# Hybrid SSD/gMLP step on one core: splits of v spread over more turns, x·dt·decay made on VectorE, weight sums begun later, product evictions at a higher priority, and four smaller moves

## The chip, the core and the metric

The kernel runs on one NeuronCore of a Trainium2 chip. The metric is the device time of one execution in microseconds (us). A core has five engines with a queue of instructions each: TensorE (PE in the rows, its weight loads PEld), VectorE (DVE), ScalarE (ACT), GpSimd (POOL) and SyncE (SP), which here only issues DMAs. Each works its own list of instructions in order and waits on semaphores for the others.

## The reference, cut to what matters

One layer, `DEPTH = 1`, over a prompt of 4096 rows and a sample of 32 rows, width 1024, all in f32:

```python
h = rms_norm(x, g_pre) * (1 + scale[:, None]) + shift[:, None]
z, xbc, dt_raw, u, v, gt = jnp.split(h @ w_in, [i1, i2, i3, i4, i5], axis=-1)
xbc, conv_new = causal_conv(xbc, conv_prev, conv_w, conv_b)      # width 4, then silu
dt = jax.nn.softplus(dt_raw + dt_bias)
y, ssm_new = ssd_scan(xs, dt, a, bm, cm, ssm_prev)               # 16 heads of 64, state 128
ssd_out = (y + d_skip[:, None] * xs).reshape(bsz, L, SSD_WIDTH) * jax.nn.silu(z)
v_n = layer_norm(v, g_v, beta_v)
gmlp_out = jax.nn.silu(gt) * u * gmlp_spatial(v_n, w_s, b_s)     # 8 groups of 128 channels
mix = jnp.concatenate([ssd_out, gmlp_out], axis=-1) @ w_out
out = x + gate[:, None] * rms_norm(mix, g_post)
```

Inside the scan a chunk's contribution to the state is `einsum(B, decay_end * dt, x)`, and the part within the chunk is `einsum((C·B) * decay, dt * x)`.

## The kernel before, in words

**Blocks and steps.** The prompt is worked in 8 blocks of 512 rows (`NB`, block index b). A block has a first step (k = 0, which makes B and C), then the output products of the block before (`out_proj`), then the products that make v (`v_stage`), then eight more steps (k = 1 to 8), each of which makes two column tiles from `w_in`: pairs of heads ("p", x and z) and groups of the gMLP branch ("g", gate and u). The sample's 32 rows ride along in block 3, and with block 4's output products. Blocks 0 and 1 use plain products (`plain_step`, `v_plain`); from block 2 on (`FROM`) the steps are done with seven products on sums of parts of the matrices instead of eight (`super_step`, `STEPS`, `LEAVES`). Every f32 operand is held as two f16 parts, and a product is three f16 products; `split` makes the two parts (ACT copies the high part, POOL or DVE subtracts for the low one).

**Weights.** In block 0 the weights are loaded in f32, scaled, split and written back to DRAM as f16 tiles. The sums of parts that the later blocks need are made in block 1 by 22 jobs (`sums_load`, `sums_scale`, `sums_first`, `sums_second`, `sums_third`, `sums_split`): DMA in, some sums on DVE, splits on ACT and POOL or DVE, DMA out from POOL's queue.

**Turns and priorities.** The order of the work is written out by hand: `later(n, fn)` puts a function n turns ahead, and `tick()`, called some 14 to 16 times in a step, starts whatever is due. What a function emits then has its place in the program; a list scheduler orders each engine's instructions by that place (the priority) among those that it holds to be ready by its own estimates. `shifted(n, fn)` emits at a priority moved by n places (negative is earlier), `behind` is `shifted(200)`, used for the sums. What the scheduler writes is then fixed: on the chip each engine keeps that order.

**A pair of heads.** When its product leaves PSUM, `conv` makes xsT on DVE (L815, L818) and `silu` follows on ACT (L805). `pair_xt` turns it on PE into rows (ps_xt, L1152). `pair_xdt` multiplies by dt on DVE (xdt<-ps_xt), one turn later `pair_xde` multiplies xdt by the decay on POOL (xde<-xdt, both L1167). `pair_state` (ps_s, L1175) needs xde; `pair_y` (ps_y, L1208) needs xdt and the masked decay L, which comes from a DMA'd row (L1124), Relu and Exp on ACT (L1134, L1139) and the mask on POOL (L1145).

**v.** `v_norm` finds mean and scale of the rows, then for chunk c of four `later(3 * c, v_split)` and per half of 512 columns `v_split_half`: vt on DVE (L1078), one turn later `split` (ACT L274, POOL L275). Half 0 is first needed by group 0 in step 2, half 1 by group 4 in step 6.

**Products leaving PSUM.** In `super_step` `leave` copies a finished product with its scale on ACT (L731), or adds it on DVE (L729); the next product but one into the same PSUM bank has to wait for it. In `plain_step` ACT does so (L757).

**Others that the change touches.** The start's bound `a_sc`, from the largest |gcol| and |scol| (L644 to L663: six DVE steps, a transpose and a product on PE, four more on DVE). `out_proj`'s end of a half: the sample's product is turned back to rows (`by_token`) right behind it, L967 to L970, and then all streams leave PSUM (L1414, L1416). `finish` for the prompt (conv and SSM states, L1435 to L1454), emitted ahead of the last `finalize_mix`. The start turns of the 22 sums jobs, `places` (L1634, L1635).

Of the kernel before, what the change touches and what calls it, by code (L numbers as in the profile page):

```python
# [18 lines left out]
P = 128  # L19
# [57 lines left out]
def hybrid_step_kernel(ctx: ExitStack, tc: tile.TileContext, io: dict, out: list):  # L77
# [566 lines left out]
    bnd = const.tile([P, 2, KT], F32, name="bnd")  # L644
    bnd2 = const.tile([P, 2, KT], F32, name="bnd2")
    nc.vector.tensor_scalar(bnd, gcol, math.sqrt(DM), None, op0=ALU.mult)
    nc.vector.tensor_single_scalar(bnd.bitcast(I32), bnd.bitcast(I32), 0x7FFFFFFF, op=ALU.bitwise_and)
    nc.vector.tensor_single_scalar(bnd2.bitcast(I32), scol.bitcast(I32), 0x7FFFFFFF, op=ALU.bitwise_and)
    nc.vector.tensor_tensor(bnd, bnd, bnd2, op=ALU.add)
    bmx = const.tile([P, 1], F32, name="bmx")  # L650
    nc.vector.tensor_reduce(bmx, bnd, axis=AX.XY, op=ALU.max)
    ps = psum("ps_bmx")
    nc.tensor.transpose(ps[0:1, 0:P], bmx, ident)
    bm1 = const.tile([1, 1], F32, name="bm1")
    nc.vector.tensor_reduce(bm1, ps[0:1, 0:P], axis=AX.X, op=ALU.max)
    nc.vector.tensor_scalar_max(bm1, bm1, 2.0 ** -40)
    ps = psum("ps_bm1")
    nc.tensor.matmul(ps[:, 0:1], ones[0:1, :], bm1, start=True, stop=True)
    e_i = const.tile([P, 1], I32, name="e_i")
    nc.vector.tensor_copy(e_i.bitcast(F32), ps[:, 0:1])  # L660
    nc.vector.tensor_single_scalar(e_i, e_i, 23, op=ALU.logical_shift_right)
    nc.vector.tensor_scalar(a_sc.bitcast(I32), e_i, -B23, (127.0 + 12 + 127) * B23, op0=ALU.mult, op1=ALU.add)
    nc.vector.tensor_scalar(a_inv.bitcast(I32), e_i, B23, -12.0 * B23, op0=ALU.mult, op1=ALU.add)  # L663
# [60 lines left out]
    def leave(s, ps, dst, scale):  # L724

        j, t, adds = LEAVES[s]
        d, sc = dst(j, t), scale(j)
        if adds:
            nc.vector.scalar_tensor_tensor(d, ps, sc, d, op0=ALU.mult, op1=ALU.add)  # L729
        else:  # L730
            nc.scalar.activation(d, ps, AF.Identity, scale=sc)  # L731
# [4 lines left out]
    def plain_step(k):  # L736

        ws = None
        for j in (1, 0):
            ps = [psum("ps_proj") for _ in range(2)]  # L740
            for kh in range(2):
# [3 lines left out]
                for pi in range(2):  # L745
# [9 lines left out]
                    if kh:  # L755
                        c = 4 * k + 2 * pi + j
                        nc.scalar.activation(ws[pi].d[j], ps[pi], AF.Identity, scale=scw[:, c:c + 1])  # L757
                        done(prompt, ws[pi], j)
# [114 lines left out]
    def dt_cumsum(st, e):  # L873
# [17 lines left out]
        nc.scalar.activation(st.de, st.de, AF.Exp)  # L891
        later(9, dt_rows, st)
# [152 lines left out]
    def v_norm(st, mv):  # L1045
# [15 lines left out]
        for c in range(n):  # L1061
            later(3 * c, v_split, st, c, mv, r)
# [4 lines left out]

    def v_split(st, c, mv, r):
        Q = st.Q
        sp = st.v[c].bitcast(F16).rearrange("p (h a d) -> p h a d", h=2, a=2)  # L1070
        for half in range(2):
            later(half, v_split_half, st, c, half, sp, mv, r)
        st.vsplit.append(sp)

    def v_split_half(st, c, half, sp, mv, r):
        Q = st.Q
        t = tmp2(prompt, "vt")[0:Q]
        nc.vector.tensor_scalar(t, st.v[c][0:Q, half * 512:half * 512 + 512], mv[0:Q, c, 0:1],  # L1078
                                r[:, c:c + 1], op0=ALU.subtract, op1=ALU.mult)
        later(1, split, sp[0:Q, half, 0], sp[0:Q, half, 1], t, nc.gpsimd)  # L1080
# [75 lines left out]
    def pair_xdt(st, j, w, ps):  # L1156
        Q, n, nm = st.Q, st.nch, st.name
        w.xdt = wk.tile([P, n, P], F32, tag="xdt" + nm, name="xdt", bufs=1)[0:Q]
        pair_times(st, j, nc.vector, w.xdt, ps[0:Q, 0:n * P].rearrange("q (c m) -> q c m", c=n), st.dt)
        later(1, shifted, -150, pair_xde, st, j, w)  # L1160

    def pair_xde(st, j, w):
        w.xde = wk.tile([P, st.nch, P], F32, tag="xde" + st.name, name="xde", bufs=1)[0:st.Q]
        pair_times(st, j, nc.gpsimd, w.xde, w.xdt, st.de)
# [215 lines left out]

    def out_proj(active, first, final=False):
# [7 lines left out]
        for half in range(1 if final else 2):  # L1389
# [4 lines left out]
            for st in active:  # L1394
                ps[st] = [psum("ps_out") for _ in range(st.nch)]
            if sample in active:
                ps_t = psum("ps_outT")
            for k2 in range(8):
# [6 lines left out]
                if k2 < 7:  # L1405
                    yield
            if sample in active:
                by_token(ps[sample][0], ps_t[:, 0:4 * TS], ps_t[:, 4 * TS:8 * TS])
            for st in active:
                if half == 0:  # L1410
                    st.o = [big("o") for _ in range(st.nch)]
                for c in range(st.nch):
                    osl = st.o[c][0:st.Q, half * 512:half * 512 + 512]
                    nc.scalar.activation(osl, ps[st][c][0:st.Q], AF.Square,  # L1414
                                         accum_out=st.os[0:st.Q, c, half:half + 1])
                    nc.scalar.activation(osl, ps[st][c][0:st.Q], AF.Copy)  # L1416
# [183 lines left out]
    for b in range(NB):  # L1600
# [30 lines left out]
        if b == 1:  # L1631

            f = region(0, "sums").rearrange("p i a k t -> p (i a k t)").bitcast(F32)
            places = [(18 + 18 * n, f[:, 0:3072]) for n in range(10)]  # L1634
            places += [(27 + 18 * n, f[:, 3072:6144]) for n in range(9)]  # L1635
# [39 lines left out]
    finish(prompt, conv_p[0, 0])  # L1675
    for st in prev:
        finalize_mix(st)
    tick()
# [33 lines left out]
```

## Time and profile before

| | |
|---|---|
| median of 3 runs | 3073.78 us (3070.44 to 3076.58) |
| the profiled execution: its own time | 3074.91 us |
| its span in the trace | 3073.2 us |
| mean granted TensorE clock | 0.972 |
| busy: PE / DVE / ACT / POOL | 92% / 57% / 50% / 42% |

The span runs from the first to the last instruction; 1.7 us lie around it. A granted clock of 1 is 2.4 GHz, one of 0.5 is 1.2 GHz. Idle time of an engine that is not the bottleneck costs nothing by itself. In the rows "L778" is line 778 of the kernel, "ps_s<-xde,bt" is what an instruction writes and reads by the program's names.

### The profile page before, as it was taken

What the parts mean: (1) busy time and instruction counts of PE and PEld (TensorE: products, weight loads), DVE (VectorE), ACT (ScalarE), POOL (GpSimd) and SP (SyncE); (2) the same over time, 40 slices, a digit from 0 to 9 for tenths busy, and PEclk for the clock granted to TensorE, in tenths of its full rate; (3) what the DMA queues carried; (4) which work ended last, traced back from release to release, by engine and by line L of the source; (5) the groups of instructions that cost most, each with busy time, mean ns of one, the idle gap of its engine ahead of it and who ended that gap; (6) DMA issues with size and microseconds to landing.
All of it is one profiled execution on the core that took longest, in us unless ns stands there. A gap on an engine that the chain in (4) does not pass through costs nothing.

```text
span 3073.2 us, 54218 instructions
## 1 busy us (share of the span) xinstructions
PE 2830.3 (92%) x20754; PEld 1881.3 (61%) x20754; DVE 1746.7 (57%) x3808; ACT 1529.6 (50%) x3234; POOL 1281.7 (42%) x1193
## 2 busy tenths in 40 slices
PE   7989898688999999989998999999999999999987
PEld 2434443344655887458874588747885588648863
DVE  4768686775664556355564554735455544526452
ACT  4577654567653554436544355444544354415531
POOL 2456654576632443224542245323543254204540
PEclk8999999899999999999999999999999999999999
DMA  9766468876435665265562666546663666556652
GB/s 316 237 211 199 146 203 297 267 240 212 151 104 201 200 195 177 90 205 178 179 201 75 215 201 195 176 155 211 192 214 102 222 195 188 182 173 198 197 159 57
DMA packets 269053, 577.36 MB, mean 188 GB/s; under 512 B 27898, under 2 KB 115170, under 8 KB 268792
## 3 DMA queue, kind: packets, MB, share of 16 engines
q1 hardware_dynamic: 246840, 500.86, 51.5%
q0 software_dynamic: 21952, 73.04, 6.4%
q8 instruction: 162, 2.65, 0.4%
q14 instruction: 99, 0.81, 0.1%
HBM read 499.82 MB, written 73.97 MB: 187 GB/s over the span
## 4 chain that ended last, share of the span: by engine, by line
PE 42%; DVE 12%; ACT 8%; DMA 5%; POOL 5%; issue 2%; SPq 0%; POOLq 0%; ACTq 0%; DVEq 0%
PE ps_proj L778 18%; PE ps_out L951 11%; PE ps_v L1016 5%; DMA wm<-vd 2%; DVE ms L1289 2%; DMA L<-acdp 2%; PE ps_y L1208 2%; PE ps_s L1175 1%; DVE vt L1078 1%; PE ps_out L1375 1%; POOL acc L1102 1%; POOL mix L1242 1%; PE ps_o L1212 1%; ACT L805 1%; DMA E<-acdp 1%
## 5 line engine op out<-in xcount | busy, mean ns | idle before, releaser
L778 PE MATMUL ps_proj<-hTp,wt 128*128 128x256 f16 x9072 | 1047.4, 274 | 44.6 <-ACT zs L731 26.5
L778 PEld LDWEIGHTS <-wt 128*128 128x128 f16 x9072 | 887.6, 98 | 157.2 <-issue 41.2
L951 PE MATMUL ps_out<-wm,mix 128*128 128x512 f16 x2880 | 646.2, 382 | 29.3 <-DVE dep L889 15.3
L951 PEld LDWEIGHTS <-mix 128*128 128x128 f16 x2880 | 280.9, 98 | 356.7 <-issue 28.1
L749 PE MATMUL ps_proj<-hTp,wt 128*128 128x512 f16 x1728 | 401.8, 389 | 2.5 <-DMA wt<-wd 2.5
L749 PEld LDWEIGHTS <-wt 128*128 128x128 f16 x1728 | 171.3, 100 | 203.0 <-issue 20.1
L1134 ACT ACTIVATE L<-L,acp 128x128 f32<-128x128 f32 x512 | 166.8, 391 | 165.6 <-DMA L<-acdp 150.5
L1016 PE MATMUL ps_v<-wm,hTp 128*128 128x512 f16 x1008 | 222.6, 381 | 17.8 <-DMA wm<-vd 17.8
L1224 POOL TENSOR_TENSOR mix<-mix,E 128x512 f32<-128x512 f32 x64 | 95.5, 1492 | 308.4 <-DVE E L1220 308.4
L1145 POOL TENSOR_TENSOR L<-L,cb 128x512 f32<-128x512 f32 (+1 forms) x144 | 168.1, 1180 | 104.7 <-ACT L L1139 103.0
L729 DVE SCALAR_TENSOR_TENSOR xp<-ps_proj,scw,xp 128x256 f32<-128x256 f32 x132 | 62.4, 480 | 233.5 <-PE ps_proj L778 221.5
L1016 PEld LDWEIGHTS <-hTp 128*128 128x128 f16 x1008 | 98.7, 98 | 139.2 <-issue 22.1
L818 DVE SCALAR_TENSOR_TENSOR xsT<-xp,cols,xsT 128x512 f32<-128x512 f32 (+1 forms) x216 | 182.8, 849 | 1.7
L275 POOL TENSOR_TENSOR mix<-ms,mix 128x512 f16<-128x512 f32 x64 | 90.8, 1421 | 220.6 <-ACT mix L274 220.6
L1102 POOL TENSOR_TENSOR acc<-acc,sq 128x512 f32<-128x512 f32 (+1 forms) x126 | 148.3, 1178 | 43.9 <-ACT sq L1098 42.4
L275 POOL TENSOR_TENSOR v<-vt,v 128x512 f16<-128x512 f32 (+1 forms) x66 | 83.7, 1297 | 174.9 <-ACT v L274 174.8
L275 POOL TENSOR_TENSOR hTp<-ta,hTp 128x512 f16<-128x512 f32 x60 | 71.3, 1189 | 202.7 <-ACT hTp L274 202.6
L810 ACT ACTIVATE halo_p<-xp 128x3 f32<-128x3 f32 x96 | 19.5, 203 | 220.5 <-DVE xp L729 219.9
L1167 POOL TENSOR_TENSOR xde<-xdt,dep 128x512 f32<-128x512 f32 x64 | 70.8, 1107 | 138.1 <-DVE xdt L1167 129.2
L274 ACT ACTIVATE mix<-ms 128x512 f16<-128x512 f32 x128 | 79.5, 627 | 83.4 <-DVE ms L1289 82.7
L1175 PE MATMUL ps_s<-xde,bt 128*128 128x128 f32 (+1 forms) x528 | 79.5, 296 | 41.2 <-POOL xde L1167 41.2
L1098 ACT ACTIVATE sq<-mix 128x512 f32<-128x512 f32 x120 | 74.8, 626 | 78.4 <-POOL mix L1242 59.0
(428 smaller groups left out, 4703.9 us busy)
## 6 DMA issues: line engine op xcount, KB each, us to landing
wt<-wd SPq DMA_DIRECT2D x414, 512.0 KB, 4.1
wm<-od SPq DMA_DIRECT2D x104, 512.0 KB, 3.5
wm<-vd SPq DMA_DIRECT2D x92, 512.0 KB, 4.9
L<-acdp SPq DMA_DIRECT2D x128, 256.0 KB, 4.1
sums<-in_w_in_dram SPq DMA_DIRECT2D x38, 512.0 KB, 6.5
wd<-wt POOLq DMA_DIRECT2D x36, 512.0 KB, 4.8
stg<-in_w_in_dram SPq DMA_DIRECT2D x64, 256.0 KB, 5.2
E<-acdp SPq DMA_DIRECT2D x128, 128.0 KB, 4.4
```

Of the source, the lines that this page charges most:

```text
L274: nc.scalar.activation(hi, src, AF.Copy)
L275: eng.tensor_tensor(lo, src, hi, op=ALU.subtract)
L749: nc.tensor.matmul(ps[pi].rearrange("p (h t) -> p h t", h=2), wt[:, pi, a, q * P:(q + 1) * P], prompt.h[:, 2 * kh:2 * kh + 2, b, q, :], st ...
L778: nc.tensor.matmul(ps, wt[:, pi, a, q * P:(q + 1) * P], prompt.h[:, slot, b, q, :], start=(starts and h == 0 and n == 0), stop=(n == 11), ...
L818: nc.vector.scalar_tensor_tensor(dst, xp[:, k:k + Ts], w(k), dst, op0=ALU.mult, op1=ALU.add)
L951: nc.tensor.matmul(ps[c], x(kk, a, c), w[:, kk, b, :], start=(first and n == 0), stop=(last and n == 5))
L1016: nc.tensor.matmul(ps, prompt.h[:, slot, a, q, i * P:(i + 1) * P], wt[q // 2][:, q % 2, b, :], start=(starts and n == 0), stop=(n == 11), ...
L1102: eng.tensor_tensor(st.accb if last else st.acc, st.acc, sq, op=ALU.add)
L1134: nc.scalar.activation(L[:, c, :], L[:, c, :], AF.Relu, scale=-1.0, bias=st.ac[:, c, 2 * j + hh:2 * j + hh + 1])
L1145: nc.gpsimd.tensor_tensor(w.L[hh], w.L[hh], st.cb[j // 4][0:st.Q], op=ALU.mult)
L1175: nc.tensor.matmul(ps_s[:, c * P:(c + 1) * P], st.bt[j // 4][0:st.Q, c, :], w.xde[:, c, :], start=True, stop=True)
L1224: nc.gpsimd.tensor_tensor(w.m, w.m, w.E, op=ALU.add)
```

## The change

It has eight parts. (1) `pair_xdt` makes both products on DVE straight from PSUM: xde first, with dd = decay times dt, which `dt_cumsum` makes with one multiply in place in `st.de`, then xdt; `pair_xde` on POOL goes. (2) The splits of v are put at turns 4(c + 4·half) for the prompt (0 to 28; 0 and 4 for the sample), halves 0 of all chunks first, and the split two turns behind vt instead of one. (3) `leave` and `plain_step`'s ACT copies are emitted with `shifted(-200)`. (4) The 19 sums jobs of region 0 start at turns 40 to 184 and 48 to 176, each 16 apart, instead of 18 to 180 and 27 to 171, each 18 apart. (5) `out_proj` emits the sample's turning back three turns later at the first half (at once at the second), and the prompt leaves PSUM without it. (6) The prompt's `finish` comes 8 turns later, behind `finalize_mix`. (7) The bound at the start is the root of a sum of squares: two ACT squares with accumulation, one add, one cast, one product on PE, four DVE steps. (8) The sample's ps_out tile is taken from PSUM only when it is turned back.

```diff
-    bnd = const.tile([P, 2, KT], F32, name="bnd")
...
-    nc.vector.tensor_scalar(a_sc.bitcast(I32), e_i, -B23, (127.0 + 12 + 127) * B23, op0=ALU.mult, op1=ALU.add)
-    nc.vector.tensor_scalar(a_inv.bitcast(I32), e_i, B23, -12.0 * B23, op0=ALU.mult, op1=ALU.add)
+    sq2 = const.tile([P, 2], F32, name="sq2")
+    sqj = const.tile([P, 2, 2 * KT], F32, name="sqj")
+    for i, (t, f) in enumerate(((gcol, math.sqrt(2 * DM)), (scol, math.sqrt(2.0)))):
+        nc.scalar.activation(sqj[:, i], t.rearrange("p s k -> p (s k)"), AF.Square, scale=f, accum_out=sq2[:, i:i + 1])
+    nc.vector.tensor_tensor(sq2[:, 0:1], sq2[:, 0:1], sq2[:, 1:2], op=ALU.add)
+    pow2_of_ssq(ssq_total(sq2[:, 0:1]), [P, 1], "wp", a_sc, a_inv)
@@ leave
-            nc.vector.scalar_tensor_tensor(d, ps, sc, d, op0=ALU.mult, op1=ALU.add)
+            shifted(-200, nc.vector.scalar_tensor_tensor, d, ps, sc, d, ALU.mult, ALU.add)
-            nc.scalar.activation(d, ps, AF.Identity, scale=sc)
+            shifted(-200, nc.scalar.activation, d, ps, AF.Identity, 0.0, sc)
@@ plain_step
-                        nc.scalar.activation(ws[pi].d[j], ps[pi], AF.Identity, scale=scw[:, c:c + 1])
+                        shifted(-200, nc.scalar.activation, ws[pi].d[j], ps[pi], AF.Identity, 0.0, scw[:, c:c + 1])
@@ dt_cumsum
+        nc.vector.tensor_tensor(st.de, st.de, st.dt, op=ALU.mult)
+        st.dd = st.de
@@ v_norm, v_split_half
-            later(3 * c, v_split, st, c, mv, r)
+            for half in range(2):
+                later((4 if st is prompt else 1) * (c + 4 * half), v_split_half, st, c, half, sp, mv, r)
-            later(half, v_split_half, st, c, half, sp, mv, r)
-        later(1, split, sp[0:Q, half, 0], sp[0:Q, half, 1], t, nc.gpsimd)
+        later(2, split, sp[0:Q, half, 0], sp[0:Q, half, 1], t, nc.gpsimd)
@@ pair_xdt
-        pair_times(st, j, nc.vector, w.xdt, ps[0:Q, 0:n * P].rearrange("q (c m) -> q c m", c=n), st.dt)
-        later(1, shifted, -150, pair_xde, st, j, w)
-        pair_times(st, j, nc.gpsimd, w.xde, w.xdt, st.de)
+        src = ps[0:Q, 0:n * P].rearrange("q (c m) -> q c m", c=n)
+        pair_times(st, j, nc.vector, w.xde, src, st.dd)
+        pair_times(st, j, nc.vector, w.xdt, src, st.dt)
@@ out_proj
+    def sample_out(half, ps_t):
+        ps = psum("ps_out")
+        by_token(ps, ps_t[:, 0:4 * TS], ps_t[:, 4 * TS:8 * TS])
+        out_leave(sample, half, [ps])
...
-                by_token(ps[sample][0], ps_t[:, 0:4 * TS], ps_t[:, 4 * TS:8 * TS])
+                later(3 if half == 0 else 0, sample_out, half, ps_t)
+            out_leave(prompt, half, ps[prompt])
@@ sums, end
-            places = [(18 + 18 * n, f[:, 0:3072]) for n in range(10)]
-            places += [(27 + 18 * n, f[:, 3072:6144]) for n in range(9)]
+            places = [(40 + 16 * n, f[:, 0:3072]) for n in range(10)]
+            places += [(48 + 16 * n, f[:, 3072:6144]) for n in range(9)]
-    finish(prompt, conv_p[0, 0])
     for st in prev:
         finalize_mix(st)
+    later(8, finish, prompt, conv_p[0, 0])
```

`out_leave` holds the two ACT instructions per chunk that `out_proj` had inline (a square with accumulation and a copy).

## Rows read from the trace of the kernel before

**Rows 1.** The page: busy us, share of the span and instructions by engine.
```profile
PE 2830.3 (92%) x20754; PEld 1881.3 (61%) x20754; DVE 1746.7 (57%) x3808; ACT 1529.6 (50%) x3234; POOL 1281.7 (42%) x1193
```
**Rows 2.** Waits of PE, whole span: who, whom; us in total, times, longest.
```profile
PE ps_s L1175 <- POOL xde L1167: 41.2, 11, 6.6
PE ps_xt L1152 <- ACT xsT L805: 38.1, 7, 22.6
PE ps_proj L778 <- ACT zs L731: 26.5, 21, 1.7
...
PE ps_out L951 <- DVE dep L889: 15.3, 4, 12.7
PE ps_out L970 <- DVE byt L968: 8.9, 2, 8.1
...
PE ps_proj L778 <- DVE xp L729: 7.1, 5, 1.4
...
PE ps_f L1440 <- DVE hk L1438: 5.7, 1, 5.7
```
**Rows 3.** Windows of blocks 0 and 1: busy us by engine, granted clock, DMA share, GB/s.
```profile
0.00:395.00 395.00, 350.55 (x1785) 168.11 (x1786) 271.50 (x565) 255.39 (x524) 206.83 (x204) 0.94 0.68 220
395.00:830.00 435.00, 364.81 (x1933) 185.28 (x1932) 312.86 (x514) 258.12 (x443) 249.29 (x253) 0.93 0.70 229
```
**Rows 4.** Waits of PE in block 1 (395 to 830 us).
```profile
PE ps_s L1175 <- POOL xde L1167: 27.1, 5, 6.6
```
**Rows 5.** Timeline, a pair of block 0: start, us, instruction, [idle before <-releaser].
```profile
221.88 0.68 DVE L1167 TENSOR_TENSOR xdt<-ps_xt,dtp 128x512 f32<-128x512 f32 x1
...
228.45 0.80 PE L1175 MATMUL ps_s<-xde,bt 128*128 128x128 f32 x2 [5.38 <-POOL xde L1167]
```
**Rows 6.** Timeline, a pair of block 1.
```profile
661.52 0.68 DVE L1167 TENSOR_TENSOR xdt<-ps_xt,dtp 128x512 f32<-128x512 f32 x1
...
663.39 0.97 PE L1175 MATMUL ps_s<-xde,bt 128*128 128x128 f32 x5 [4.58 <-POOL xde L1167]
```
**Rows 7.** Instructions of line 1167: count, duration ns min/median/max, first and last start.
```profile
L1167 DVE TENSOR_TENSOR xdt<-ps_xt,dtp x64: 678/692/693, 181.0 to 2940.2; 128x512 f32<-128x512 f32 x64
L1167 POOL TENSOR_TENSOR xde<-xdt,dep x64: 1037/1049/1492, 183.2 to 2943.2; 128x512 f32<-128x512 f32 x64
```
**Rows 8.** Timeline of block 1 behind the products of v.
```profile
604.95 0.67 ACT L757 ACTIVATE xp<-ps_proj,scw 128x512 f32<-128x512 f32 x1
...
612.68 1.11 PE L1152 MATMUL ps_xt<-ident,xsT 128*128 128x128 f32 x4 [22.63 <-ACT xsT L805]
```
**Rows 9.** Instructions of line 1078, as in rows 7.
```profile
L1078 DVE TENSOR_SCALAR vt<-v,mvp,nrp x64: 529/1366/5212, 153.0 to 2781.6; 128x512 f32<-128x512 f32 x64
```
**Rows 10.** Timeline of block 1's output products.
```profile
471.70 2.72 PE L951 MATMUL ps_out<-wm,mix 128*128 128x512 f16 x6 [12.66 <-DVE dep L889]
```
**Rows 11.** Window of block 1, sums tiles alone: busy DVE, ACT, POOL, then as rows 3.
```profile
395.00:830.00 435.00, 112.05 (x133) 67.53 (x95) 91.29 (x114) 0.93 0.70 229
```
**Rows 12.** Timeline of a step of block 5.
```profile
2188.65 5.40 PE L778 MATMUL ps_proj<-hTp,wt 128*128 128x256 f16 x48
...
2195.28 0.46 ACT L731 ACTIVATE zs<-ps_proj,scw 128x256 f32<-128x256 f32 x1
...
2195.78 1.47 PE L778 MATMUL ps_proj<-hTp,wt 128*128 128x256 f16 x12 [1.73 <-ACT zs L731]
```
**Rows 13.** Timeline of block 5 behind the products of v.
```profile
2095.30 7.95 DVE L1078 TENSOR_SCALAR vt<-v,mvp,nrp 128x512 f32<-128x512 f32 x8
...
2114.11 0.70 PE L1152 MATMUL ps_xt<-ident,xsT 128*128 128x128 f32 x4 [2.10 <-ACT xsT L805]
```
**Rows 14.** Timeline of the start.
```profile
47.10 0.17 DVE L640 SCALAR_TENSOR_TENSOR gcol<-gcol,cols 128x16 f32<-128x16 f32 x1
...
55.41 0.14 DVE L662 TENSOR_SCALAR a_sc<-e_i 128x1 int32<-128x1 int32 x1
```
**Rows 15.** Timeline of the end, ahead of the last output products.
```profile
2966.04 1.91 PE L1451 MATMUL ps_f<-ident,Hp 128*128 128x128 f32 x8
```

More of the change, by code (lines that the diff above doesn't have):

```diff
@@ L642, in hybrid_step_kernel @@
                                    op0=ALU.add, op1=ALU.mult)
-    bnd = const.tile([P, 2, KT], F32, name="bnd")
[L645 to L661, printed above, removed]
-    nc.vector.tensor_scalar(a_sc.bitcast(I32), e_i, -B23, (127.0 + 12 + 127) * B23, op0=ALU.mult, op1=ALU.add)
-    nc.vector.tensor_scalar(a_inv.bitcast(I32), e_i, B23, -12.0 * B23, op0=ALU.mult, op1=ALU.add)
+    sq2 = const.tile([P, 2], F32, name="sq2")
[4 more added lines that the diff above has]
+    pow2_of_ssq(ssq_total(sq2[:, 0:1]), [P, 1], "wp", a_sc, a_inv)
     nc.vector.tensor_scalar(gcol, gcol, a_sc, None, op0=ALU.mult)
@@ L1061, in v_norm @@
         for c in range(n):
-            later(3 * c, v_split, st, c, mv, r)
+            sp = st.v[c].bitcast(F16).rearrange("p (h a d) -> p h a d", h=2, a=2)
+            st.vsplit.append(sp)
+            for half in range(2):
+                later((4 if st is prompt else 1) * (c + 4 * half), v_split_half, st, c, half, sp, mv, r)
         if st is sample:
@@ L1066, in v_norm @@
                 later(4 + 2 * g, sample_spatial, g)
[L1068 to L1071, printed above, removed]
-            later(half, v_split_half, st, c, half, sp, mv, r)
-        st.vsplit.append(sp)
     def v_split_half(st, c, half, sp, mv, r):
@@ L1157, in pair_xdt @@
         Q, n, nm = st.Q, st.nch, st.name
-        w.xdt = wk.tile([P, n, P], F32, tag="xdt" + nm, name="xdt", bufs=1)[0:Q]
-        pair_times(st, j, nc.vector, w.xdt, ps[0:Q, 0:n * P].rearrange("q (c m) -> q c m", c=n), st.dt)
-        later(1, shifted, -150, pair_xde, st, j, w)
-    def pair_xde(st, j, w):
-        w.xde = wk.tile([P, st.nch, P], F32, tag="xde" + st.name, name="xde", bufs=1)[0:st.Q]
-        pair_times(st, j, nc.gpsimd, w.xde, w.xdt, st.de)
+        w.xdt, w.xde = [wk.tile([P, n, P], F32, tag=t + nm, name=t, bufs=1)[0:Q] for t in ("xdt", "xde")]
+        src = ps[0:Q, 0:n * P].rearrange("q (c m) -> q c m", c=n)
+        pair_times(st, j, nc.vector, w.xde, src, st.dd)
+        pair_times(st, j, nc.vector, w.xdt, src, st.dt)
     def pair_times(st, j, eng, dst, src, f):
@@ L1379, in out_last_half, with out_leave @@
             yield
+    def out_leave(st, half, ps):
+        for c in range(st.nch):
+            osl = st.o[c][0:st.Q, half * 512:half * 512 + 512]
+            nc.scalar.activation(osl, ps[c][0:st.Q], AF.Square, accum_out=st.os[0:st.Q, c, half:half + 1])
+            nc.scalar.activation(osl, ps[c][0:st.Q], AF.Copy)
+    def sample_out(half, ps_t):
+        ps = psum("ps_out")
+        by_token(ps, ps_t[:, 0:4 * TS], ps_t[:, 4 * TS:8 * TS])
+        out_leave(sample, half, [ps])
     def out_proj(active, first, final=False):
@@ L1393, in out_proj @@
                     st.gp = gate_row(st)
-            for st in active:
-                ps[st] = [psum("ps_out") for _ in range(st.nch)]
+            ps[prompt] = [psum("ps_out") for _ in range(prompt.nch)]
             if sample in active:
@@ L1406, in out_proj @@
                     yield
+            if half == 0:
+                for st in active:
+                    st.o = [big("o") for _ in range(st.nch)]
             if sample in active:
-                by_token(ps[sample][0], ps_t[:, 0:4 * TS], ps_t[:, 4 * TS:8 * TS])
[L1409 to L1416, printed above, removed]
+                later(3 if half == 0 else 0, sample_out, half, ps_t)
+            out_leave(prompt, half, ps[prompt])
             if half == 0:
```

## The prediction

> **What bounds the kernel now.** I read the page first: PE is busy 92% of the span, the next engine 57% [rows 1], so PE's list sets the time, and what can be won without taking work from it are its idle 243 us (3073.2 − 2830.3) and the products that it runs at the lower clock. Second the waits of PE: they say who ended its idle time. Seven lines hold 143 of the 243 us [rows 2], and each names something that the change touches: xde from POOL 41.2, xsT from ACT 38.1, evictions by ACT 26.5 and by DVE 7.1, a small PSUM read in the output products 15.3, the sample's turning back 8.9, the states at the end 5.7. Third the windows by stage: blocks 0 and 1 take 830 us and hold 115 us of the idle time, at granted clocks of 0.94 and 0.93 of 2.4 GHz, with DVE at 69 and 72% [rows 3]. Last the timeline around each long wait, to see which instruction was late and why; what follows stands on that.
>
> **xde on DVE (16 pairs of blocks 0 and 1, 48 later).** PE waits for xde 11 times, all before block 2: 27.1 us in five waits in block 1 [rows 4], so 14.1 us in six in block 0. In block 0 DVE had xdt ready long before: in the pair shown at 222.56, PE got xde at 228.45 after a wait of 5.38, because POOL had other work [rows 5]. With xde made where xdt stands now, the product can start with it; of the six I count all 14.1 (bounds 0 and 14.1). In block 1 DVE itself is late: xdt ends at 662.20 and PE starts at 663.39, so a DVE xde in xdt's place takes only 1.2 of 4.58 us [rows 6]. The five waits give between 5 × 1.1 (POOL's own 1.05 at least) and 27.1; I take 10, nearer to the lower one since rows 6 is the usual picture there. The price: xdt from PSUM takes 678 to 693 ns in all 64 cases, POOL's xde 1037 to 1492 [rows 7], so DVE gets 64 × 0.69 = 44 us more and POOL loses at least 67 (64 × 1.05). From block 2 on DVE has room (57% over the span); in blocks 0 and 1, 16 × 0.69 = 11 us lie on an engine that is often late. Cost 5 (0 to 11). xdt, one instruction later, is not needed before ps_y. The multiply that makes dd is one instruction of 128x64 per block, and the sample's pairs are small: nothing, hidden in DVE's idle time.
>
> **v's pieces spread, evictions earlier.** Behind the products of v PE stood 22.63 us in block 1, until xsT of the next pair was ready. The products that feed it had ended at 590.05 (612.68 − 22.63), but ACT copied them out only from 604.95 on, 15 us later [rows 8]: ahead of that copy in its list stood v's splits, which waited for vt, and DVE's vt took a median of 1366 ns where the fastest took 529 [rows 9]. Both edits aim at this place: the copy goes up 200 places, the splits go back by up to 28 turns. The conv of four DVE instructions, silu and a table load still lie between, some 6 us, so I take 16 (0 to 22.6). In the later blocks the same place costs less: eight vt hold DVE for 7.95 us, then PE waits 2.10 us for xsT [rows 13]. The other six waits for xsT hold 15.5 us (38.1 − 22.6) and DVE's late additions 7.1 [rows 2]; of 22.6 I take 12 (0 to 22.6), since ACT's rows also come late there by DMA.
>
> The third place is in every step: PE ran 48 products from 2188.65 and then waited 1.73 us for a copy that ACT did at 2195.28 [rows 12]. The copy belongs to the second quarter or third of those products, ready by 2192.7 at the latest; ACT did decay work first. That is the row of 26.5 us in 21 waits [rows 2]. With 200 places of lead the copy stands ahead of it whenever the scheduler holds it to be ready. I take 18 (0 to 26.5). What is queued behind the copies loses 0.47 us each and has PE's whole step as cover.
>
> **Sums later.** PE stood 12.66 us in block 1's output products until DVE had read the small ps_ac [rows 10]; DVE and ACT stood in sums and in the new output weights. The first job now starts 22 turns later, so less of it lies ahead of that read: 8 (−10 to 12.7). But 19 of the jobs now start every 8 turns on the mean instead of every 9, and end 4 turns later. They cost DVE 112 us in block 1 [rows 11], 5.9 a job, and move that load by about 12% into the steps where DVE is late already. Cost 8 (0 to 30).
>
> **The three small moves.** The sample's turning back: 8 of the 8.9 us [rows 2] (0 to 8.9), as PE then has the second half's products to run in the three turns. The states at the end: nine transposes, 1.91 us for the eight of them, stand ahead of the sum that the last products wait for [rows 15]; behind it they cost PE about half of that, and DVE two copies less in the chain: 2 (0 to 5.7). The start: from gcol to a_sc 8.1 us [rows 14], twelve instructions that hop between DVE and PE, each of a tenth or two of a us with weight splits in between; about nine are left. 3 (0 to 5).
>
> **Clock.** Behind each of the longer waits the granted clock is low: 0.93 over block 1 is 30 us of 435 not granted, 0.94 over block 0 is 24 [rows 3]. Most of that lies inside the waits themselves. What goes with them I take at 10 (0 to 25).
>
> **A new order.** The priorities change some 900 evictions, and all lists are written anew by estimates that no row shows. The nearest row is the wait of 1.26 us (26.5/21) that a step has now [rows 2]; one in each of the 48 steps would be 60. Cost 15 (0 to 60).
>
> **Sum.** Gains 14.1 + 10 + 16 + 12 + 18 + 8 + 8 + 2 + 3 + 10 = 101; costs 5 + 8 + 15 = 28. Net 73. The profiled execution took 3074.9 (1.7 around its span), 1.1 above the median: 3074.9 − 73 = **3002 us**. The bounds alone run from 2905 (170 of gains, no cost) to 3186 (101 of costs, 10 lost); the cases below narrow that.
>
> **Rivals.**
> *Order edits do little.* On the chip each engine keeps a list that was written for other times; a copy 200 places earlier helps only if the scheduler saw it ready. For it: ACT's list already put those copies behind work that was itself waiting. Then 14.1 + 10 + 8 + 2 + 3 and 5 of the clock remain, less 15: 27 us, 3048.
> *Everything goes.* All listed waits end and only 45 of the costs come: 170 − 45 = 125, 2950. Against it: block 1's late DVE [rows 6].
> *The pieces of v in POOL's way.* vt has 529 ns at best and 1366 in the median [rows 9], xdt never more than 693 [rows 7]: vt is slowed by something else. Spread out, 8 pieces in 8 blocks could each cost (1366 − 529) on the path of a pair, 54 us, leaving 19: 3056. Against it: they run beside POOL's work now, too, and POOL has 58% idle. The Trainium skill ("SBUF — State Buffer", Who interferes with whom) states for this that VectorE and GpSimd share a pair of ports as an exclusive lock, taken by copies and tensor_scalar in a two-port mode or by two SBUF inputs, and not by an instruction with one input from PSUM. By that rule this rival would hold, and xde from PSUM would come free of it; the spread of the two rows agrees.
> *Slower.* Place: block 1, by the denser sums. If ACT or DVE comes late as at 612.68, by 22.6 us, for four more of its eight pairs, 90 us come on top: 3074.9 − 73 + 90 = 3092. It decides from 73 us on, more than three such stalls. For it: DVE at 72%, POOL at 57%, the DMA queues at 0.70 [rows 3]. Against it: the jobs start as late as 40 and none has to end before block 2.
> *No change.* What PE wins it waits for elsewhere, on weights: a block 1 shorter by an eighth would put the DMA share at 0.80, below full, so this needs all gains small.
>
> **How the numbers follow.** Forecast 0.45 (its own range 2975 to 3030), order edits of little use 0.22, everything 0.13, the pieces in POOL's way 0.07, no change within 0.2% (6 us, about what runs of this kernel can tell) 0.06, slower 0.07. Faster is 0.45 + 0.22 + 0.13 + 0.07 = 0.87. The range 2955 to 3060 leaves out half of "everything" and the last two, 0.20.
>
> **What would show it.** Right: no wait for POOL's xde, two L1167 rows on DVE near 690 ns each; the wait of 22.6 at the head of block 1's steps under 8; the row "ps_proj <- ACT zs" under 10 us in all; none of 12.7 in the output products; the sample's wait gone; the idle time of PE near 150 us and block 0's and 1's clock at 0.96 or more. Wrong: new rows among PE's waits for xde from DVE above 20 us, for L or the masks (ps_y), or for weights; a block 1 above 420 us; or copies L731 that wait for PE with decay work queued behind, and PE then for that.

## The result and the profile after

The changed kernel takes **3034.06 us** (median of 4 runs, 3030.18 to 3035.61) where the kernel before takes 3072.11 beside it (4 runs, 3066.95 to 3076.58): a ratio of **0.9866, 95% interval 0.9853 to 0.9879**. That is 38 us where the forecast of 3002 meant 72 (3073.8 − 3002). The sign is right and the time lies inside the stated range, but outside the forecast case's own range (2975 to 3030), between it and the rival "order edits do little" (3048). The profiled execution took 3030.18 us, the fastest of the four, with a span of 3028.3, against 3074.9 and 3073.2 before.

The page's row of busy time, then the waits of PE that answer to [rows 2] (in total, times, longest; line numbers are those of the changed kernel, L381 is the helper `shifted`):

```profile
PE 2817.2 (93%) x20752; PEld 1875.0 (62%) x20752; DVE 1773.4 (59%) x3884; ACT 1524.4 (50%) x3236; POOL 1202.9 (40%) x1121
```
```profile
PE ps_proj L765 <- ACT zs L381: 26.2, 21, 1.7
PE ps_xt L1137 <- ACT xsT L792: 25.2, 7, 18.0
PE ps_out L940 <- DVE dep L876: 19.3, 5, 12.3
...
PE ps_s L1157 <- DVE xde L1149: 15.8, 5, 7.7
PE ps_ssq L300 <- DVE ssb L298: 15.0, 5, 5.9
...
PE ps_ms L1257 <- DVE accb L1087: 5.6, 1, 5.6
...
PE ps_out L959 <- DVE byt L957: 1.0, 1, 1.0
```

PE's idle time is 3028.3 − 2817.2 = 211 us, 32 less than before; its busy time is 13 less, and the two make the span's 45, 7 more than the medians differ by. The list has lost POOL's xde, the sample's 8 us (byt) and VectorE's late additions. It has not lost the copy of zs (26.5 before), nor the 12.7 for dep (12.3 now, and 19.3 in all instead of 15.3), and 18.0 of the 22.6 stand. New are xde from VectorE, ssb (the cast in front of a sum of squares, mostly of the weights' columns; 2.6 before) and accb (the last norm's sum of squares) in place of hk.

The windows of start, block 0 and block 1, each cut at the first dt product (busy us by engine, granted clock, DMA share, GB/s), answer to [rows 3]; the cut differs, so the same cut of before stands in the table below:

```profile
0.00:52.52 52.52, 36.97 (x117) 11.84 (x117) 20.00 (x80) 18.93 (x40) 12.19 (x24) 0.97 1.00 338
52.52:406.37 353.85, 327.46 (x1757) 163.32 (x1758) 269.79 (x514) 246.36 (x506) 193.65 (x178) 0.96 0.64 206
406.37:838.93 432.56, 368.51 (x2026) 193.78 (x2025) 316.23 (x536) 255.41 (x446) 237.64 (x245) 0.93 0.70 234
```

The same cut of all profiled runs, in us (the last column reaches to the span's end):

| kernel | start | block 0 | block 1 | the rest |
|---|---|---|---|---|
| before | 58.7 | 356.1 | 437.4 | 2221.0 |
| **after** | 52.5 | 353.9 | 432.6 | 2189.4 |
| one_xde | 58.3 | 351.0 | 437.0 | 2226.3 |
| one_vspread | 57.3 | 354.6 | 437.6 | 2200.3 |
| one_leaves | 57.4 | 360.0 | 439.1 | 2220.9 |
| one_sums | 58.9 | 356.2 | 441.1 | 2227.1 |
| one_bound | 54.2 | 357.9 | 440.8 | 2220.6 |
| one_outend | 55.8 | 357.0 | 434.9 | 2213.8 |
| two | 57.7 | 349.7 | 433.7 | 2196.6 |
| four | 52.6 | 350.0 | 432.1 | 2187.6 |
| four_gv | 54.4 | 352.5 | 433.5 | 2163.6 |
| four_gv_gap | 54.4 | 350.3 | 435.2 | 2154.1 |
| four_gv_cum | 53.1 | 346.5 | 435.5 | 2147.4 |
| no_adds | 52.4 | 346.2 | 419.9 | 2148.5 |

Blocks 0 and 1, where the forecast had most of its gain, gave 2.3 and 4.9 us; the start gave 6.2 and the rest 31.6. Each row is one execution, and not the median one: that of one_xde and that of four_gv took 8 us more than the median of their kernel, those of one_vspread, one_outend and no_adds 5 to 7 us less. From block 2 on every engine of four_gv and four_gv_gap has the same instructions in the same order, and yet the last column differs by 9.5 us; for before and one_sums it differs by 6. The start, in kernels that have the old one, runs from 55.8 to 58.9. So entries are read for steps larger than that, or together with the rows of waits.

### The profile page after: what moved, and what is told of

Its sections match the earlier page's. It is cut to its first block, busy times and chain, and to the rows that moved or that the text cites. A ratio compares the mean times of both kernels' runs of the same rounds, so it can differ in the third digit from the quotient of the medians.

```text
span 3028.3 us, 54218 instructions
## 1 busy us (share of the span) xinstructions
PE 2817.2 (93%) x20752; PEld 1875.0 (62%) x20752; DVE 1773.4 (59%) x3884; ACT 1524.4 (50%) x3236; POOL 1202.9 (40%) x1121
## 4 chain that ended last, share of the span: by engine, by line
PE 37%; DVE 11%; issue 8%; ACT 7%; POOL 5%; DMA 5%; SPq 0%; POOLq 0%; ACTq 0%; DVEq 0%
PE ps_proj L765 18%; PE ps_out L940 9%; PE ps_v L1005 2%; DVE ms L1271 2%; DMA L<-acdp 2%; PE ps_y L1190 2%; PE ps_s L1157 1%; PE ps_out L1357 1%; POOL mix L1224 1%; POOL mix L1213 1%; PE ps_o L1194 1%; ACT L L1119 1%; POOL acc L1087 1%; DVE bT L805 1%; DVE cT L805 1%
## 5 line engine op out<-in xcount | busy, mean ns | idle before, releaser
L940 PE MATMUL ps_out<-wm,mix 128*128 128x512 f16 x2880 | 645.7, 381 | 30.6 <-DVE dep L876 19.3
L381 DVE SCALAR_TENSOR_TENSOR xp<-ps_proj,scw,xp 128x256 f32<-128x256 f32 x132 | 62.7, 480 | 213.3 <-ACT xp L381 129.1
L1271 DVE TENSOR_TENSOR ms<-mix,sb 128x512 f32<-128x512 f32 x128 | 101.3, 805 | 17.3 <-POOL hTp L275 9.2
L1213 POOL TENSOR_TENSOR mix<-mix,us 128x512 f32<-128x512 f32 x64 | 81.9, 1283 | 47.6 <-ACT us L381 32.0
```

The source lines that it names most:

```text
L940: nc.tensor.matmul(ps[c], x(kk, a, c), w[:, kk, b, :], start=(first and n == 0), stop=(last and n == 5))
L1213: nc.gpsimd.tensor_tensor(m, m, w.d[1], op=ALU.mult)
L1271: nc.vector.tensor_tensor(t, m, sb, op=ALU.mult)
```

## Experiments: the parts alone

Each of the first six kernels is the kernel before with one part of the change; the diffs are those parts of the change shown above.

**one_xde** (xde from PSUM on VectorE). 

> The kernel before with part 1 alone: xde and xdt both made on DVE from PSUM. By the prediction's terms: 24 us of PE's waits for xde go and some 6 of the lower clock behind them, 5 come back on DVE, so about -25 us (ratio 0.992), and PE's row for xde holds some 17 us, all in block 1. The rival, read from the changed kernel, whose blocks 0 and 1 took only 7 us less in all: the waits move to the next instruction that is late, so -8 us or less (0.997 or above), blocks 2 to 7 within 1 us of before each.

Measured: 3066.34 us beside 3075.54, ratio 0.9974 (0.9962 to 0.9986). Some 9 us, not 25, close to the rival's 8. In the profile block 0 is 5 us shorter and block 1 as long as before; it is that of the slowest of twelve executions, so it shows which waits moved, but not where all of the 9 us lie. Over the whole span PE waits 21.6 us for VectorE's xde and 6.2 for ssb, where it waited 41.2 for POOL's and 2.6 for ssb:

```profile
PE ps_s L1175 <- DVE xde L1167: 21.6, 6, 7.9
```

**one_vspread** (v's pieces on turns 0 to 28). 

> The kernel before with part 2 alone: v's pieces at turns 0 to 28, their splits two turns later. By the prediction's terms: half of the 22.6 us wait at the head of block 1's steps and 12 us behind v in the later blocks, so -15 to -25 us (0.992 to 0.995). The rival: block 1's wait stays above 15 us since the copy out of PSUM and the table loads make it, and only blocks 2 to 7 gain, 3 us each with their clock: -15 to -20 us as well, but with the wait at 612 us still there and blocks 2 to 7 each 2 to 4 us shorter.

Measured: 3056.85 us, ratio 0.9946 (0.993 to 0.9961): 18.7 us, the largest single part. The time fits both the theory and the rival; the wait at the head of block 1's steps is the rival's, 18.0 us where it was 22.6, above 15. The gain stands in the last column, 20.7 us; block 1 has none. PE's waits for xsT and xp from block 2 on, 12.3 and 7.1 us before, are 3.7 and none. But POOL's xde has become later, 54.3 us in all instead of 41.2; the three rows are those of blocks 0, 1 and the rest, before 14.1, 27.1 and none:

```profile
PE ps_s L1175 <- POOL xde L1167: 19.2, 5, 7.3
...
PE ps_s L1175 <- POOL xde L1167: 31.2, 5, 7.9
...
PE ps_s L1175 <- POOL xde L1167: 3.8, 4, 1.3
PE ps_xt L1152 <- ACT xsT L805: 3.7, 5, 1.6
```

**one_leaves** (product copies 200 places earlier). 

> The kernel before with part 3 alone: the evictions 200 places earlier. By the prediction's terms: 18 of the 26.5 us that PE waits for ACT's copies in the steps, and some of block 1's 22.6: -20 to -25 us (0.992 to 0.9935). The rival: in the steps of blocks 2 to 7 the list of ACT stays as it was but for neighbours that change places, since the scheduler does not hold the copies to be ready before the decay work; the row of 26.5 us stays within 3 us, and the time is within 3 us of before (0.999 to 1.001).

Measured: 3078.08 us, ratio 1.0011 (1.0001 to 1.0021): nothing won, some 2.5 us lost. That is the rival: from block 2 on 2157 of ACT's 2245 instructions stand in the order of before. Copies passed neighbours, but in the steps they did not pass the decay work. The row that it aimed at is as it was:

```profile
PE ps_proj L778 <- ACT zs L381: 28.5, 21, 1.7
```

**one_sums** (the weight sums begun later and closer). 

> The kernel before with part 4 alone: 19 of the sums jobs begin later. By the prediction's terms: 8 us less in block 1's output products and 8 us more in its steps, so none in all (0.997 to 1.003), and the 12.7 us wait under 6. The rival: the 12.7 us wait stays, because DVE and ACT reach the small PSUM reads late for another reason than the sums; blocks other than 1 unchanged; the time within 5 us of before.

Measured: 3084.92 us, ratio 1.0028 (1.0017 to 1.0039), 9.4 us slower. The ratio lies in the range that was expected, the wait does not: for dep it is still 12.1 at the longest, and POOL's xde rose from 41.2 to 47.9. Block 1 is 3.7 us longer in the profile; where the rest of the 9.4 lies it does not show. In block 1 VectorE runs the same 527 instructions in 324.9 us instead of 308.1, in another order beside POOL's.

```profile
415.12:856.20 441.08, 367.92 (x2026) 194.05 (x2025) 324.92 (x527) 255.95 (x446) 249.45 (x253) 0.92 0.70 229
```

**one_bound** (the start's bound from sums of squares). 

> The start's bound alone (a sum of squares in place of the two maxima), all else as before. Theory: the start, from the span's begin to the first dt product, was 58.7 us before and 52.5 after the whole change, and nothing else of the change lies there, so this alone gives 5 to 7 us: 3068.5 to 3070.5 beside 3075.5 for the kernel before; PE's wait for bmx (4.2 us) is gone. Rival: the 6.2 us are made up later by weights that are not yet there in block 0 (they are loaded and split in a fixed order): less than 3 us, above 3072.5.

Measured: 3073.54 us beside 3073.97, ratio 0.9997 (0.9985 to 1.0009). The time is the rival's; its reason, weights that are late in block 0, is not shown. In the profile the start is 4.5 us shorter, and blocks 0 and 1 are 5 us longer together, a size at which a single profile can't say where the 4.5 go.

**one_outend** (the sample's turning back and the end states later). 

> The sample's turning back three turns later and the prompt's end states behind the last mix, all else as before. Theory: of the row of 8.9 us in PE's wait for byt all but 1.0 goes, as it did after the whole change, and the last block is about 2 us shorter by the states: 8 to 10 us in all, 3065.5 to 3067.5. Rival: the sample's wait goes, but the end wins nothing, since another short wait (5.6 us for accb) stood in place of the 5.7 us for hk: 6 to 8 us, 3067.5 to 3069.5. Were it under 4 us, the sample's wait would have hidden other late work.

Measured: 3069.75 us, ratio 0.9981 (0.9968 to 0.9995), 4 to 6 us, less than the theory's 8 to 10 and hardly the rival's 6 to 8. Of the sample's 8.9 us only 0.8 are left, but PE's waits for dep rose from 15.3 to 19.7: in the output products where the sample's 8.1 us stood, PE now waits 2.75 us for dep. At the end 5.6 us for accb stand where 5.7 for hk stood, so the end won nothing.

```profile
PE ps_out L951 <- DVE dep L889: 19.7, 5, 12.7
...
PE ps_ms L1275 <- DVE accb L1102: 5.6, 1, 5.6
```

By their medians the six add up to 9.2 + 18.7 − 2.5 − 9.4 + 0.4 + 4.2 = 21 us, and the whole gave 38. So some of the parts seem to help each other.

## Experiments: parts together

**two** is one_xde and one_vspread in one kernel. 

> Only xde on VectorE and v's pieces spread; the rest as before. Alone they gave 9.2 and 18.7 us; four, with the bound (0.4) and the sample and states (4.2) besides, gave 49, where the four parts alone add up to 32. Theory: these two support each other. With v spread, VectorE and POOL are even in the later blocks, where xde on VectorE alone cost about 5 us of what it won in block 0; together they give 38 to 45: 3029 to 3036 where the kernel before stands at 3074. Rival: the parts simply add, 25 to 31 us, 3043 to 3049, and the rest of four's gain comes from the start or the sample standing beside them.

Measured: 3035.28 us beside 3075.52, ratio 0.9867 (0.9846 to 0.9889): 40 us where the two alone give 28. The two do support each other. PE's waits for xde are 54.3 us with the spread alone and 17.7 here (2.6 in block 0, 15.1 in block 1): the spread had added 13 us to them, and with xde on VectorE that price is gone. That these 13 are the 12 us beyond the sum is not shown: as far as the table can say, most of what the two give beyond their sum stands in the last column, where the spread had added 3.8 of the 13, and none in block 0, where it had added 5. These two edits alone are worth as much as the whole change.

```profile
PE ps_s L1175 <- DVE xde L1167: 17.7, 5, 6.9
```

**four** is the whole change without the edits of one_leaves and one_sums. 

> The whole change without two of its edits: product evictions at their old priority and the sums at their old turns; so xde on VectorE, v's pieces spread, the bound, the sample and the end states. Alone, the evictions cost 2.5 us and the sums 9.4. Theory: they cost the same within the whole, so this kernel stands about 12 us under the whole change: 3022 to 3027 where the kernel before stands at 3075. Rival: the denser sums only cost where xde is POOL's work; with xde on VectorE they cost nothing, and this kernel stands where the whole change does, 3034 to 3040. If it is slower than that, the later sums did help as the prediction had it.

Measured: 3025.09 us beside 3073.97, ratio 0.9843 (0.9823 to 0.9863). By the ratios this is 7 us under the changed kernel, by the differences of the medians 11; the intervals of the two kernels just overlap, so that the two edits cost within the whole what they cost alone is likely, not certain. No run shows that either helps.

**four_gv** tests why the copy of zs is late in every step. A step of block 5 after the change shows it (start, us, instruction, [idle before <-releaser]); it is the stretch of [rows 12], some ten us earlier:

```profile
2181.24 1.27 POOL L1224 TENSOR_TENSOR mix<-mix,mx 128x512 f32<-128x512 f32 x1
...
2182.54 0.63 ACT L1083 ACTIVATE sq<-mix 128x512 f32<-128x512 f32 x1 [1.38 <-POOL mix L1224]
2183.08 0.68 ACT L1119 ACTIVATE L<-L,acp 128x128 f32<-128x128 f32 x2
...
2183.78 1.28 ACT L1124 ACT_TABLE_LOAD   x1
2185.07 0.63 ACT L1124 ACTIVATE L<-L 128x512 f32<-128x512 f32 x1
2185.61 0.46 ACT L381 ACTIVATE zs<-ps_proj,scw 128x256 f32<-128x256 f32 x1
...
2186.11 1.47 PE L765 MATMUL ps_proj<-hTp,wt 128*128 128x256 f16 x12 [1.45 <-ACT zs L381]
```

ACT's order is that of before: square, decay work, table load, copy. ACT stands 1.38 us in the square, because POOL makes the group's product only then, and PE waits 1.45. The edit gives that product to VectorE from block 2 on and leaves ACT's order there alone:

```diff
 def group_mixed(st, g, m, mx):
-    (nc.vector if st.end and g == 7 else nc.gpsimd).tensor_tensor(m, m, mx, op=ALU.mult)
+    (nc.gpsimd if st.pl else nc.vector).tensor_tensor(m, m, mx, op=ALU.mult)
```

> The kernel called four, with one more edit: from block 2 on, the product of a group's mix with its spatial part is VectorE's instead of POOL's. ScalarE's list stays the same; only what its square waits for comes sooner. Theory of the wait in each step: the copy of zs is late because ScalarE stands 1.4 us in the square ahead of it, which waits for POOL's product, and not because of the copy's priority. Then the row of PE's waits for that copy falls from 26 us to under 8, and the kernel is 15 to 22 us faster than four. Rival 1: the decay work and the table load between the square and the copy (about 2.6 us) are long enough by themselves: the row stays above 18, under 6 us gained. Rival 2: VectorE's 48 added instructions of about 0.7 us make hc, xde or additions late: PE waits for VectorE rise by more than 10 us, and nothing is gained.

Measured: **2997.41 us** beside 3073.97, ratio 0.9753 (0.9731 to 0.9775), 28 us under four, more than the 15 to 22 expected. The rest of the span is 24 us shorter, and ACT's order from block 2 on is that of four. The same step now:

```profile
2166.39 6.73 PE L778 MATMUL ps_proj<-hTp,wt 128*128 128x256 f16 x60
...
2166.84 0.69 DVE L1242 TENSOR_TENSOR mix<-mix,mx 128x512 f32<-128x512 f32 x1 [1.19 <-POOL mix L1231]
...
2168.08 0.62 ACT L1099 ACTIVATE sq<-mix 128x512 f32<-128x512 f32 x1
...
2171.14 0.46 ACT L731 ACTIVATE zs<-ps_proj,scw 128x256 f32<-128x256 f32 x1
```

The square waits for nothing, the copy starts 3.06 us behind it instead of 3.07, and PE runs 60 products on end through the place. Of PE's waits for copies by ACT in the super steps this is what is left:

```profile
PE ps_proj L778 <- ACT us L731: 0.7, 2, 0.4
```

So the row of 26 us was the wait of an instruction ahead of the copy: it went with that wait, where 200 places of priority had not moved it. Rival 2 did not come: PE's waits for xde, hc (the state from chunk to chunk) and ssb from VectorE are 37.5 us in all where four has 35.4.

**four_gv_gap** pauses the sums behind v in block 1.

```diff
-            places = [(18 + 18 * n, f[:, 0:3072]) for n in range(10)]
-            places += [(27 + 18 * n, f[:, 3072:6144]) for n in range(9)]
-            places += [(114 + 30 * n, spare(prompt.h)) for n in range(3)]
+            places = [(18 + 16 * n + 32 * (n > 4), f[:, 0:3072]) for n in range(10)]
+            places += [(26 + 16 * n + 32 * (n > 4), f[:, 3072:6144]) for n in range(9)]
+            places += [(126 + 26 * n, spare(prompt.h)) for n in range(3)]
```

> four_gv with a pause in block 1's sums: the same 22 jobs, none begun between turns 91 and 125, so none in work while v's pieces and the first pair behind v go through VectorE and ScalarE; they stand about 10% closer before and after. Theory: PE's wait of 17.5 us for xsT behind v in block 1 is made by the sums that lie there in VectorE's and ScalarE's lists, not by the priority of the copy nor by v's pieces. Then it falls below 8 and block 1 is 6 to 12 us shorter: 2986 to 2992 beside 2997 for four_gv. Rival: VectorE's whole load in block 1 is what counts, and a pause there makes longer waits elsewhere in the block: the wait falls, the block stays at 428 to 438 us, and the time is the same within 5 us.

Measured: 3000.31 us beside 3075.52, ratio 0.9755 (0.9736 to 0.9775), as four_gv. PE's waits in block 1 of four_gv, and then of four_gv_gap:

```profile
PE ps_s L1175 <- DVE xde L1167: 17.6, 3, 8.1
PE ps_xt L1153 <- ACT xsT L805: 17.5, 1, 17.5
PE ps_out L952 <- DVE dep L889: 13.2, 1, 13.2
```
```profile
PE ps_s L1175 <- DVE xde L1167: 28.9, 6, 10.5
PE ps_out L952 <- DVE dep L889: 12.6, 1, 12.6
...
PE ps_xt L1153 <- ACT xsT L805: 1.6, 1, 1.6
```

The rival: with v's pieces spread, the sums behind v do make the 17.5 us; without them there PE waits longer for xde further on, and block 1 is 435.2 instead of 433.5.

**four_gv_cum** sends ps_ac's products earlier.

```diff
-        later(24, dt_cumsum, st, e)
+        later(16, dt_cumsum, st, e)
```

> four_gv with the small products of the decay sums (ps_ac) sent 16 turns behind dt instead of 24, in every block. Theory: PE's wait of 13.2 us in block 1's output products lasts until VectorE and ScalarE, which stand in a chain of sums and output weights, have read ps_ac; its bank is needed for the second half. Sent some 10 us earlier, the reads lie in front and the bank is free in time: the wait falls below 4, 8 to 10 us gained, about 2988 beside 2997 for four_gv. Rival: the reads fall as late as before, behind the same chain, or a wait of the second half's products for their weights (wm) takes the place: less than 3 us.

Measured: **2984.51 us** beside 3075.52, ratio 0.9708 (0.9684 to 0.9731), the fastest of the kernels here that compute the reference. But not as the theory has it. In block 1 the 13.2 us are gone and others have their place:

```profile
PE ps_out L952 <- ACT o L1385: 7.8, 1, 7.8
...
PE ps_ac L882 <- DVE dtt L870: 5.3, 1, 5.3
```

Block 1 is 435.5 us, 2 longer. In the profiles the gain lies in block 0 (6) and the rest (16.2), but they differ by more (21.6) than the medians (12.9), as that of four_gv was a long one. Beside four_gv_gap, which has four_gv's lists from block 2 on, the rest is 6.7 us shorter, and that is about the 5.5 us for dep that four_gv had in the later blocks (18.7 − 13.2) and that are gone here.

**no_adds** takes the sums' additions from VectorE (four_gv_cum without the four `tensor_tensor` lines in `sums_first`, `sums_second` and `sums_third`; the splits take the scaled parts instead).

```diff
-        nc.vector.tensor_tensor(w.t, a21, a22, op=ALU.add)
-        nc.vector.tensor_tensor(a21, a11, a21, op=ALU.subtract)
...
-        nc.vector.tensor_tensor(w.t, w.t, a11, op=ALU.subtract)
...
-        nc.vector.tensor_tensor(w.t, w.a[:, 512:1024], w.t, op=ALU.subtract)
```

> four_gv_cum without VectorE's additions and subtractions in the 22 sums jobs of block 1 (88 instructions of 128x512; the sums' weights are then plain scaled parts, so the later blocks compute something else with the same instructions). In four_gv_cum these hold VectorE for about 80 us of the block's 435, and it stands 22 us behind POOL in one of them. Theory: PE's idle time in block 1 (62 us), which no edit so far brought down by more than 9 and which moved from place to place, hangs on the work of the sums on VectorE. Without it PE's idle time there is under 40 and the block is 15 to 30 us shorter: 2955 to 2970 beside 2984.5. Rival: it is the hops between engines and the transfers of the sums, or the rest of the block's own chain, that make PE wait; then the block is 428 or more, and the time within 7 us of 2984.5.

Measured: 2974.49 us beside 3076.24, ratio 0.9671 (0.9648 to 0.9694), 10 under four_gv_cum. Block 1 of four_gv_cum and of no_adds (busy us of PE, PEld, DVE, ACT and POOL, then as above):

```profile
399.55:835.02 435.47, 373.27 (x2026) 195.04 (x2025) 323.26 (x540) 254.28 (x445) 237.21 (x243) 0.92 0.70 230
```
```profile
398.63:818.53 419.90, 367.25 (x2027) 192.35 (x2026) 242.80 (x451) 256.37 (x448) 229.30 (x241) 0.94 0.71 238
```

VectorE has 80.5 us less and the block is 15.6 shorter, at the low end of the theory's 15 to 30; the time stays above its 2955 to 2970, and below the rival's. PE's idle time there, length less busy, goes from 62.2 to 52.7, not under 40. PE's waits for xde in block 1, 15.4 us before, are 2.3; those that are left are again for xsT, hc and the second half's bank:

```profile
PE ps_xt L1153 <- ACT xsT L805: 17.9, 2, 14.4
PE ps_o L1212 <- DVE hc L1197: 11.4, 3, 5.5
PE ps_out L952 <- DVE acT L902: 9.1, 1, 9.1
```

So the additions are one part of block 1's length: 0.12 us (by the medians) to 0.19 us (by the profiles) for each us of VectorE's work. Without them the jobs also have fewer hops between engines, so load and hops are not told apart. What the larger part hangs on, the order of the lists, the transfers or the block's own chain, stays open.

## Why the prediction was right in sign and short in size

- **xde, block 0 (14.1) and block 1 (10, cost 5): the right event, the wrong worth.** POOL's xde is off the list, xde and xdt take 691 and 681 ns in the median as forecast, and in block 0 PE waits 2.1 us for xde where it waited 14.1. But the two blocks became 7.2 us shorter in all, from everything, and one_xde, for which the terms make 19, gave 9. In block 0 PE now waits 12.2 us for ssb, 2.6 before (6.2 in one_xde), VectorE's part in the scaling of weights; in block 1 the waits move on along the list, as four_gv_gap and four_gv_cum show. The step that failed is "of the six I count all 14.1": it took a wait that ends as time won, with VectorE at 69 and 72% busy and the next wait close behind it.
- **The head of block 1's steps (16 of 22.6):** 4.6 went, and block 1 won none of it in one_vspread. The step that failed is "ahead of that copy in its list stood v's splits, which waited for vt": they did, but VectorE's list had sums between the vt. With v's pieces spread 18 us stayed, and with the sums out of the way 1.6 (four_gv_gap). The place before the change:

```profile
593.02 1.64 DVE L412 TENSOR_SCALAR sums<-sums,sw 128x1024 f32<-128x1024 f32 x1
...
596.14 1.37 DVE L1078 TENSOR_SCALAR vt<-v,mvp,nrp 128x512 f32<-128x512 f32 x1
597.43 1.64 DVE L417 TENSOR_TENSOR sums<-sums 128x512 f32<-128x512 f32 x1
597.54 0.63 ACT L274 ACTIVATE v<-vt 128x512 f16<-128x512 f32 x1 [3.52 <-DVE vt L1078]
```

- **Later blocks behind v (12): the right place, too small.** Of the 22.6 us of waits in that term (3.1 of them in block 0), 3.7 are left in one_vspread, and the rest of the span is 20.7 us shorter. That VectorE is free sooner is a small part of it. vt (count, then ns min/median/max, against [rows 9]) has a median of 547 ns instead of 1366, but its times are of two kinds. Before, 30 of the 64 vt took under 0.6 us and 34 over 0.8; after, 36 and 28. The median jumps from one kind to the other, and all 64 together fell from 67.4 to 56.6 us.

```profile
L1063 DVE TENSOR_SCALAR vt<-v,mvp,nrp x64: 527/547/2745, 149.9 to 2776.5; 128x512 f32<-128x512 f32 x64
```

  The rival "pieces of v in POOL's way" was right in its mechanism and wrong in its price. Every one of the 34 long vt before, and of the 28 after, starts while POOL is in an instruction; of the 30 and 36 short ones 27 and 35 start while it is in none. So vt is slow where it meets POOL at work, in its new turns too; but PE's waits behind v went all the same, and the 54 us did not come. The Trainium skill ("SBUF — State Buffer", Who interferes with whom) has VectorE and GpSimd exclude each other in such pairs of instructions. For vt the trace agrees, by these counts. xde and xdt, which read PSUM, show nothing of it: none of the 128 took over 693 ns, and 74 of them started with POOL at work. On POOL's side the spread has a price that the rival did not name: alone it made PE's waits for xde 13 us longer, of which the 3.8 us from block 2 on stand right behind v's splits in POOL's list.
- **Copies at a higher priority (18): wrong, 0.3.** The step that failed is "with 200 places of lead the copy stands ahead of it whenever the scheduler holds it to be ready". It did not stand ahead of it, neither after the change nor in one_leaves. The rival "order edits do little" was right on this part, and four_gv shows that an instruction ahead of the copy set that wait.
- **Sums later (8, cost 8):** the wait of 12.7 was 12.3 after, so nothing was won; alone the edit costs 9.4, near the cost of 8 that was forecast. VectorE's instructions did take 17 us longer in block 1, but of the 9.4 only 3.7 stand there in the profile. The rival that ended slower named the place; the four further stalls of 22.6 us that it priced did not come.
- **Small moves:** the sample's wait went as forecast, but a wait for dep took part of its place, and one_outend gave 4 to 6 us where the sample and the end were put at 10; the end gave nothing, accb in place of hk. The start is 6.2 us shorter in the profile of after, and 4.4 in the mean of the seven profiles with the new bound against the seven with the old, where 3 were forecast; alone it left no trace in the time.
- **Clock (10):** PE's busy time fell by 13 us, but elsewhere than forecast: 4.3 in the start, where the granted clock rose from 0.88 to 0.97, 8.4 behind block 1, and 0.4 in blocks 0 and 1 together, from which the term was worked out and whose clock stayed at 0.96 and 0.93.
- **New order (15):** no row shows it as such. one_leaves, which moves the 900 evictions alone, cost 2.5 us; later ssb and hc may belong to it too.

So the terms were wrong in both directions, and that their sum fell inside the range is in part luck: xde, the head of block 1, the copies and the sums gave far less than was counted, and the spread of v in the later blocks gave more.

Of what was to be seen, three things came (xde's two rows, POOL's wait gone, the sample's wait gone) and five did not (22.6 under 8, zs under 10, none of 12.7, PE's idle time near 150, block 1's clock of 0.96); block 0's clock of 0.96 stood there before, in this cut. Of the signs of being wrong one came: block 1 is above 420 us, at 432.6 (437.4 before).

## What to carry to other kernels

A wait that goes is worth its length only if the engine behind it has room up to the next wait. In a stage like block 0 or 1 here, where VectorE was about 70% busy, count a part, and look which instruction is late next. When a copy comes late, read its engine's list upward to the first instruction that itself waited; moving that one's source (28 us here) helped where the copy's priority (2.5 us lost) did not. Where one edit makes a queue later and another takes work out of that queue, measure them together as well: 9 and 19 us alone, 40 as a pair. Before reading a median, look whether the times are of two kinds. And compare a profile's stages only as far as two executions of the same lists agree: here to 9.5 us at the widest.

## What the runs showed of the hardware

- Two kinds of VectorE instruction that read only SBUF were slow where POOL was in an instruction when they started. vt (128x512 in f32) took at most 0.55 us in 30 of 64 cases before the change, and 0.8 us or more, mostly 1.37, in the other 34, which all started that way. The 128x512 product that four_gv moved took 0.68 to 0.69 us in 33 of its 50 cases, and 0.93 to 1.74 in the 17 others, which all started that way; its mean is 0.90.
- The two products of a pair that read PSUM did not show this: after the change none of the 128 took over 0.69 us, and 74 of them started with POOL at work.
- The same 527 VectorE instructions of block 1 took 308.1 us before and 324.9 in one_sums, where they stand in another order beside POOL's.
